# A hybrid MLA and FoX attention layer on one core: nine more places for raw weights during the half-block products, and a new schedule for the sums of w_out's blocks

## The chip, the cores and the metric

One core of a Trainium2 chip runs the kernel; the other cores of the chip are not used. The time of a run is the device time of one execution in microseconds. Before the change three runs took 912.26, 913.48 and 908.7 us, the median is 912.26 us. The profiled execution took 912.14 us, of which the profile's span covers 910.4 us, with a granted TensorE clock of 0.997.

## The reference

One decoder layer with S = 512 positions and D = 2048 columns: an RMS norm, one wide input projection, two attention branches of eight heads each (latent attention, "MLA", and forgetting attention, "FoX"), both with SiLU gates, one output projection, a second RMS norm and the residual.

```python
h = _rms_norm(x, g_pre)
proj = h @ w_in
(q_lat, kv_lat, k_rope_raw, gate_mla,
 fq, fk, fv, f_logit, gate_fox) = jnp.split(proj, split_points, axis=-1)
o_mla = _mla_branch(q_lat, kv_lat, k_rope_raw, g_q, w_uq, g_kv, w_ukv, cos, sin) * jax.nn.silu(gate_mla)
o_fox = _fox_branch(fq, fk, fv, f_logit, b_forget) * jax.nn.silu(gate_fox)
o = jnp.concatenate([o_mla, o_fox], axis=-1) @ w_out
return x + _rms_norm(o, g_post)
```

Both branches are causal softmax attention; FoX adds differences of cumulated forget gates to its logits, MLA gets its heads' queries, keys and values from normed latents by two more projections.

## The kernel before

**Matmuls and chunks.** Every float32 product is made of three matmuls of split operands: the weights' high part by the activations' high part, low by high, and high by low (`mm3`, L137 to L140). A weight matrix is streamed in chunks of 128 x 1024 float32 (0.524 MB). For each chunk SP issues one load into a `raw` tile (`load`), ScalarE casts it to the high part (`whi`, L249), VectorE subtracts this from raw and gets the low part (`wlo`, L250, a "division"), and TensorE takes both. `chunk(i)` loads up to four chunks ahead and divides two ahead. `raw` has three places in the pool `wp`, so a load waits until the third chunk before it is divided.

**The stages**, by chunk number: the FoX heads and, last of them, the projection of the rest of the latents (`lat`, up to 72, its matmuls take 408 to 435 us together with the tails of the last two FoX heads); then the half-block products 73 to 128; the MLA heads 129 to 148; w_out from 149 on.

**The half-block products.** The latents' (`l`) and the MLA gate's (`m`) projections are computed with fewer block products from sums of blocks: p1, p2, p4, then q6, g5, g7, g3. Each product has four chunks for `l` (matmul tiles gl, gbl, then gcl, gdl) and four for `m` (gm, gbm, gcm, gdm): 73 to 76 p1 l, 77 to 80 p1 m, 81 to 88 p2, 89 to 92 p4 l, 93 to 96 p4 m, 97 to 128 the rest. Chunks 89 to 96 are made of two loads: `raw` from a sum in DRAM (t6) and `second` from w_in; VectorE adds them (L246) right before the division.

**Sums of blocks.** The sums are made in DRAM, one step each, 56 in all (`add_step`): SP copies the first block into a tile `t` (L297), POOL accumulates the second block into it with a DMA (L294), and SP writes a mark of 16 numbers from a weight tile into the next `t` (L299), which ties the step to the progress of the products. `paced` starts a step after as many weight blocks as `set_pace` says: every 4 in `lat`, none in the half-block products (1000), every 2 in the MLA heads.

**Other traffic.** POOL writes attention outputs and their gate sums out to DRAM (`awayoa`, `awayog`, `put` at L884), SP fetches operands of products back (`fetch`, L908: bmq, bmg; boa).

**Pools.** `pp` holds the attention heads' own tiles (two places of each), `tb` and `tp` constants and temporary tiles. `inner`, which holds all three, is closed before the output's pool `op` opens, which takes their room.

**Order.** The program is written in TensorE's order; side work (the `todo` queue) is taken out of a queue between matmul groups, `rate` pieces at a time (`pump`). A scheduler then orders the instructions of each engine by its own costs. Each engine and each DMA queue then runs its instructions in that fixed order.

Of the kernel before, what the change touches and what calls it, by code (L numbers as in the profile page):

```python
# [12 lines left out]
F32 = mybir.dt.float32  # L13
# [6 lines left out]
P = 128  # L20
# [22 lines left out]
RND = 12582912.0  # L43
V3 = 3 * HW
NSLOT = 28


def split_const(c, bits, n):
# [15 lines left out]
def tile_hybrid_layer(  # L64
# [16 lines left out]
    nc = tc.nc  # L81
# [5 lines left out]

    inner = ctx.enter_context(ExitStack())
    tb = inner.enter_context(tc.tile_pool(name="tb", bufs=1))
    pp = inner.enter_context(tc.tile_pool(name="pp", bufs=2))  # L90
    tp = inner.enter_context(tc.tile_pool(name="tp", bufs=4))
    dr = ctx.enter_context(tc.tile_pool(name="dr", bufs=1, space=bass.MemoryType.DRAM))
    ps = ctx.enter_context(tc.tile_pool(name="ps", bufs=4, space=bass.MemoryType.PSUM))

    def slot(name, dt=F32, shape=(P, 2, S)):

        return sp.tile(list(shape), dt, tag="s", name=name)
# [4 lines left out]
    def proj_bank(name):  # L102
        return bank("pj", name, 4)
# [90 lines left out]
    chunks = []  # L194
# [11 lines left out]

    raws, ready = {}, {}

    more = []

    def raw_tile(i):
        pool = more[0] if more and (i - more[1]) % 6 < 3 else wp
        return pool.tile([P, 1024], F32, tag="raw", name=f"raw{i}", bufs=3)

    def load(i, small=None):

        w, cols, k, n, width = chunks[i]
        if cols is None:

            raw = raw_tile(i)  # L220
            nc.sync.dma_start(raw, w)
            raws[i] = raw
            if k is not None:
                second = slot(f"second{i}")
                nc.sync.dma_start(second, k)
                raws[i] = raw, second.rearrange("p k c -> p (k c)")
            return
        if i < 2:
            raw = slot(f"raw{i}", shape=(P, 1024))
        else:  # L230
            raw = raw_tile(i)
        v = raw[:, : n * width].rearrange("p (k c) -> p k c", k=n)
        for at, off, cnt in cols:
            (nc.sync if cnt >= P or small is None else small).dma_start(
                v[:, :, at : at + cnt],
                w[0, k * P : (k + n) * P, off : off + cnt].rearrange("(k p) c -> p k c", p=P),
            )
        raws[i] = raw
# [14 lines left out]
    state = {"loaded": 0, "divided": 0, "tiles": 0, "turn": 0, "step": -1, "pace": 6}  # L253
# [4 lines left out]
            state["divided"] += 1  # L258

    def chunk(i, ahead_load=4, ahead=2):  # L260
        while state["loaded"] < min(len(chunks), i + ahead_load + 1):
            load(state["loaded"])
            state["loaded"] += 1
        prepare(i + ahead)
        return ready.pop(i)

    fox = []
    for p in range(4):
        c = {}
# [13 lines left out]
    lat = add_chunks(w_in, [(0, 1024, 256)], NK, 4, 256)  # L283
# [197 lines left out]
    def set_pace(n):  # L481
        state.update(pace=n, tiles=0)
# [17 lines left out]
    def proj_T(rng, outs, kh, kl, rate=1):  # L500

        k = 0
        n_k = sum(chunks[i][3] for i in rng)
        for i in rng:
            hi, lo = chunk(i)
            for j in range(chunks[i][3]):
                for o, rows, pick in outs:
                    mm3(o[:rows, :], pick(hi, j), pick(lo, j), kh[k], kl[k], k == 0, k == n_k - 1)
                k += 1
                pump(rate)  # L510
                behind(hi)
# [406 lines left out]
    def along(a, b):  # L918
        return [lambda x=x, y=y: (x(), y()) for x, y in zip(a, b)]
# [4 lines left out]
    def operand(n, of):  # L924
        def parts(kk, t):
            return [oper[n, of][kk // 2][:, x, kk % 2, t * P : (t + 1) * P] for x in range(2)]

        return parts
# [256 lines left out]
        latents[i] = split(raw(i), f"ln{i}")  # L1185

    todo.append(rotary_key)
    set_pace(4)
    lb = [proj_bank(f"l4{i}") for i in range(2)]
    proj_T(lat, [(lb[i], P, two[i]) for i in range(2)], hh, hl)  # L1190
    while later:
        later.popleft()()
    for i in range(2):
# [15 lines left out]
    def sums_wide(n):  # L1209
        return lambda kk: [oper[n, "m"][kk // 2][:, x, kk % 2, :] for x in range(2)]  # L1210
# [30 lines left out]
    def gate(f, top, bottom):  # L1241

        if f % 2 == 0:
            o_of.append(slot(f"gm{f // 2}"))
        g = o_of[-1][:, f % 2, :]
        pt = att_bank(f"gmt{f}")
        c = slice(f % 4 * P, (f % 4 + 1) * P)
        for t in range(NT):
            pe.transpose(pt[:, t * P : (t + 1) * P], (top, bottom)[t // 2][:, t % 2, c], ident)
        act.activation(g, pt, AF.Tanh)  # L1250
        dve.scalar_tensor_tensor(out=g, in0=g, scalar=1.0, in1=pt, op0=ALU.add, op1=ALU.mult)
        gm.append(g)

    set_pace(1000)
    A, A2 = ([proj_bank(f"g{n}{t}") for t in range(2)] for n in "lm")
    product("p1", "l", x_wide(0, 0), A, True, True, turned=True)
# [22 lines left out]
    scaled(c21, B2, 2, pb)  # L1279
    drain()  # L1280
    C, G = ([proj_bank(f"g{n}l{t}") for t in range(2)] for n in "cd")
    product("q6", "l", sums_wide("q6"), C, True, True, side=[*f5[2:], *along(d5[:2], f7[:2])], turned=True)
    raws_of += [slot(f"lat{i}") for i in (2, 3)]
    lat_sum(lat_block(1, 0), C, pl, ALU.subtract)
# [34 lines left out]
    drain()  # L1319
    for f in range(4, 8):  # L1320
        todo.append(lambda f=f: gate(f, c12, c22))
    qnh, qnl = zip(*(latents[i] for i in range(6)))
    knh, knl = zip(*(latents[i] for i in range(6, 10)))


    for p in range(4):
        c = mla[p]
        if p == 3:
            for f in (*fetches("a11", "o"), *fetches("a12", "o")):
                f()  # L1330
        qb = [proj_bank(f"mq{p}{i}") for i in range(3)]

        proj_T(c["q"], [(qb[i], P, cols(i * P)) for i in range(3)], qnh, qnl, rate=2)
        q = [[split(qb[i], f"mq{p}{i}", SC_M, first=P)] for i in range(2)]
        wholes = slot(f"mw{p}")
        qw = [[whole_block(wholes, i, qb[i], SC_M)] for i in range(2)]
        a, b = rotate(qb[2], P, SC_M, f"q{p}")
        for i in range(2):
            r = tmp(f"rq{p}{i}")
            src = slice(ROPE * i, ROPE * (i + 1))  # L1340
            for half in range(2):
                dve.tensor_tensor(
                    out=r[ROPE * half : ROPE * (half + 1), :], in0=a[src, :], in1=b[src, :], op=ALU.add
                )
            q[i].append(split(r, f"rq{p}{i}", first=P))
            qw[i].append(whole_block(wholes, 4 + i, r))
        if p == 0:
            set_pace(2)
        if p == 3:
            todo.extendleft([*divisions("a11", "o"), *divisions("a12", "o")])  # L1350
        kb = [proj_bank(f"mk{p}{i}") for i in range(2)]
        vb = [proj_bank(f"mv{p}{i}") for i in range(2)]

        def v_cols(w, j):
            return w[:, j, :].rearrange("p (h c) -> p h c", h=2)[:, :, NOPE:]

        kk = 0
        for i in c["kv"]:
            hi, lo = chunk(i)
            for j in range(chunks[i][3]):  # L1360
                fst, lst = kk == 0, kk == KVR // P - 1
                for n in range(2):
                    w = cols(256 * n)
                    mm3(kb[n], w(hi, j), w(lo, j), knh[kk], knl[kk], fst, lst)
                for t in range(NT):
                    o = vb[t // 2][:, (t % 2) * 256 : (t % 2) * 256 + 256]
                    ts = slice(t * P, (t + 1) * P)
                    mm3(
                        o, knh[kk][:, ts], knl[kk][:, ts], v_cols(hi, j), v_cols(lo, j),
                        fst and t % 2 == 0, lst, skip_group_check=True,  # L1370
                    )
                kk += 1
                pump(2)
                behind(hi)
        k = [[split(kb[i], f"mk{p}{i}"), (kr, None)] for i in range(2)]
        kw = [[whole_block(wholes, 2 + i, kb[i]), kr.bitcast(F32)[:, :P]] for i in range(2)]
        drain()
        values_into(v_pair(f"mv{p}"), slice(0, 256), [piece_of(vb, t, 256)[0] for t in range(NT)])
        vs = values_of(f"mv{p}")
        heads = [  # L1380
            Head(
                f"m{2 * p + i}", q[i], k[i],
                vs[i],
                lambda h=2 * p + i: gm[h],
                list(zip(qw[i], kw[i])),
            )
            for i in range(2)
        ]
        enqueue_scores(heads)
        enqueue_values(heads)  # L1390
        done += heads
# [124 lines left out]
            s()  # L1516

    product("p2", 0, operand("a12", "o"), A, False, True, 2, (6, heads_end))
    inner.close()
    op = ctx.enter_context(tc.tile_pool(name="op", bufs=8, reuse_waits="tile"))  # L1520
    more.extend([op, state["loaded"]])
# [88 lines left out]
```

## Time and profile before

| What | us |
|---|---|
| median of three runs | 912.26 |
| lowest and highest | 908.7, 913.48 |
| the profiled execution | 912.14 |
| its span | 910.4 |
| TensorE busy in it | 898.7 |
| VectorE busy | 625.2 |
| ScalarE busy | 424.6 |
| p1, p2 and p4 (chunks 73 to 96) run on TensorE from, to | 436, 505 |
| q6 to g3 (chunks 97 to 128) run from, to | 505, 601 |

TensorE works in 4732 matmuls. A matmul of 512 columns starts 0.23 us after the one before it, one of 256 columns 0.12 us; a larger distance is a wait. In the rows of the trace PE is TensorE, DVE VectorE, ACT ScalarE, and SPq the queue of DMA issues on SP. `out<-in` names the tiles, and a bracket at the end of a row says how long the engine had been idle and what ended that. DMA shares are the mean over the core's 16 DMA engines; 1 is all busy.

### The profile page before, as it was taken

Reading aid. Unit: us, or ns where it says so; the run is one execution under the profiler, and the core shown is the slowest. Engines: PE = TensorE matmul, PEld = TensorE weight load, DVE = VectorE, ACT = ScalarE, POOL = GpSimd, SP = SyncE. Lnnn points to the kernel's source line nnn. Section 1 sums busy time; section 2 is a strip of 40 time slices with the busy share of each in tenths; the row PEclk is TensorE's granted clock in tenths of the full one; section 3 lists DMA queues with packets and bytes.
Section 4 is the critical chain, followed back from the end, with each engine's and each line's share of the span. In section 5 each row is a group of like instructions: output and inputs, shape, how many; then the busy total and the mean of one; then the engine's idle time right before and its main releaser. Section 6 shows DMA issues by size and latency. Waiting matters only on the chain.

```text
span 910.4 us, 12934 instructions
## 1 busy us (share of the span) xinstructions
PE 898.7 (99%) x4732; PEld 774.3 (85%) x4732; DVE 625.2 (69%) x1074; ACT 424.6 (47%) x779; POOL 80.9 (9%) x97
## 2 busy tenths in 40 slices
PE   8999999999999999999999999999999999999997
PEld 8988888898889988888998998878888888888885
DVE  3467778537563684474758777978877986886585
ACT  5773333234222342242464556644554565654483
POOL 1010110110120110111100000001101000000021
PEclk9999999999999999999999999999999999999998
DMA  9378987987898798899798875559999546786878
GB/s 291 96 197 192 250 218 199 231 222 195 231 256 210 200 233 226 228 219 228 228 312 304 289 221 162 162 157 230 215 231 254 117 122 203 243 257 216 278 188 251
DMA packets 121364, 199.40 MB, mean 219 GB/s; under 512 B 16050, under 2 KB 59596, under 8 KB 121300
## 3 DMA queue, kind: packets, MB, share of 16 engines
q1 hardware_dynamic: 105044, 158.84, 55.5%
q0 software_dynamic: 15520, 39.33, 23.5%
q8 instruction: 37, 0.61, 0.3%
q10 hardware_dynamic: 736, 0.40, 0.2%
q14 instruction: 27, 0.22, 0.1%
HBM read 186.46 MB, written 70.80 MB: 283 GB/s over the span
## 4 chain that ended last, share of the span: by engine, by line
PE 92%; DVE 4%; DMA 2%; ACT 1%; issue 1%; SPq 0%; ACTq 0%; DVEq 0%
PE fv L561 4%; PE fg L138 3%; PE fq L140 3%; PE fq L138 3%; PE fq L139 3%; PE fg L140 3%; PE fg L139 3%; PE fk L139 3%; PE fk L140 3%; PE fk L138 3%; PE sm L604 3%; PE fv L140 2%; PE fv L138 2%; PE fv L139 2%; PE mq L138 2%; PE mq L140 2%
## 5 line engine op out<-in xcount | busy, mean ns | idle before, releaser
L250 DVE TENSOR_TENSOR wlo<-raw,whi 128x1024 fp32r<-128x1024 f32 (+3 forms) x205 | 242.8, 1186 | 172.3 <-ACT whi L249 162.2
L249 ACT CAST whi<-raw 128x1024 fp32r<-128x1024 f32 (+3 forms) x205 | 209.4, 1022 | 297.5 <-PE fk L139 52.9
L138 PE MATMUL fq<-h,whi 128*128 128x512 f32 x128 | 52.6, 411 | 0.0
L138 PE MATMUL fg<-h,whi 128*128 128x512 f32 x128 | 51.0, 398 | 0.0
L140 PE MATMUL fq<-h,wlo 128*128 128x512 f32 x128 | 50.3, 393 | 0.0
L139 PE MATMUL fq<-h,whi 128*128 128x512 f32 x128 | 50.1, 391 | 0.0
L140 PE MATMUL fg<-h,wlo 128*128 128x512 f32 x128 | 50.1, 391 | 0.0
L138 PE MATMUL fk<-h,whi 128*128 128x512 f32 x128 | 50.0, 391 | 0.0
L139 PE MATMUL fg<-h,whi 128*128 128x512 f32 x128 | 49.9, 390 | 0.0
L139 PE MATMUL fk<-h,whi 128*128 128x512 f32 x128 | 49.8, 389 | 0.0
L140 PE MATMUL fk<-h,wlo 128*128 128x512 f32 x128 | 49.8, 389 | 0.0
L294 POOL DMA_DIRECT2D t<-in_w_out_dram x16 | 18.5, 1159 | 261.8 <-DMA t<-in_w_out_dram 232.1
L140 PE MATMUL fv<-whi,h 128*128 128x256 f32 (+1 forms) x128 | 39.5, 309 | 0.0
L139 PE MATMUL fv<-wlo,h 128*128 128x256 f32 (+1 forms) x128 | 39.5, 309 | 0.0
L138 PE MATMUL fv<-whi,h 128*128 128x256 f32 (+1 forms) x128 | 39.5, 309 | 0.0
L561 PE MATMUL fv<-whi,h 128*128 128x456 f32 x128 | 38.9, 389 | 0.0
L621 ACT ACTIVATE pf<-sf,stf 128x128 f32<-128x128 f32 (+3 forms) x32 | 16.9, 528 | 26.9 <-DVE stf L619 26.9
L138 PE MATMUL mq<-ln,whi 128*128 128x512 f32 x72 | 28.8, 400 | 0.0
L140 PEld LDWEIGHTS fq<-h,wlo 128*128 128x128 f32 x128 | 24.0, 188 | 5.4
L140 PEld LDWEIGHTS fg<-h,wlo 128*128 128x128 f32 x128 | 24.0, 188 | 5.3
L139 PE MATMUL mq<-ln,whi 128*128 128x512 f32 x72 | 28.3, 393 | 0.0
L140 PEld LDWEIGHTS fk<-h,wlo 128*128 128x128 f32 x128 | 24.0, 188 | 5.0
(525 smaller groups left out, 2456.8 us busy)
## 6 DMA issues: line engine op xcount, KB each, us to landing
raw<-in_w_in_dram SPq DMA_DIRECT2D x80, 512.0 KB
t<-in_w_out_dram SPq DMA_DIRECT2D x32, 512.0 KB
raw<-t SPq DMA_DIRECT2D x32, 512.0 KB
raw<-in_w_out_dram SPq DMA_DIRECT2D x24, 512.0 KB
t<-in_w_out_dram POOLq DMA_DIRECT2D x16, 512.0 KB, 8.5
t<-t POOLq DMA_DIRECT2D x16, 512.0 KB, 7.5
awaymg<-rmg POOLq DMA_DIRECT2D x8, 512.0 KB, 8.6
raw<-t6l SPq DMA_DIRECT2D x8, 512.0 KB
```

The costliest lines, as they stand in the source:

```text
L138: pe.matmul(o, ah, bh, start=first, stop=False, **kw)
L139: pe.matmul(o, ah, bl, start=False, stop=False, **kw)
L140: pe.matmul(o, al, bh, start=False, stop=last, **kw)
L249: act.copy(hi[:, :m], raw[:, :m])
L250: dve.tensor_tensor(out=lo[:, :m], in0=raw[:, :m], in1=hi[:, :m].bitcast(F32), op=ALU.subtract)
L294: pool.dma_start(to.rearrange("p (k c) -> p k c", k=2), second, accum_op=ALU.add)
L561: pe.matmul(banks[t][:, :n], a[k][:, tss[t]], b[:, j, :], start=k == 0 and m == 0, stop=k == NK - 1 and m == 2,)
L604: pe.matmul(s[:, :nn], a[:, qs], c[:, :nn], start=(i == 0), stop=(i == len(pairs) - 1))
L621: act.activation(p, s[:, :n], AF.Exp, bias=st[:, 0:1], accum_out=st[:, 1:2])
```

## The change

The pool `pp` moves into a room of its own, `heads_room`, which is closed before the half-block products. In its place a pool `rw` with nine raw places (`DEEP`) is opened, until the MLA heads open `pp` again. In the products nine of twelve raws take a deep place, three a place of `wp`; the `second` blocks of 89 to 96 take deep places too (before: slots of the general pool). Loads run up to eleven chunks ahead in place of four. In `lat` a sum step comes after every 3 blocks in place of 4, which makes five steps there in place of four, and the side work is pumped at rate 2. From q6 on there is a step after every 8 blocks, eight steps in all (before: none). In the MLA heads the steps come after every 4 blocks in place of every 2, eight steps in place of seventeen.

```diff
+DEEP = 9
...
-    pp = inner.enter_context(tc.tile_pool(name="pp", bufs=2))
     tp = inner.enter_context(tc.tile_pool(name="tp", bufs=4))
+    heads_room = ctx.enter_context(ExitStack())
+    pp = heads_room.enter_context(tc.tile_pool(name="pp", bufs=2))
...
     def raw_tile(i):
+        if deep and deep[1] <= i < deep[2] and (i - deep[1]) % (DEEP + 3) < DEEP:
+            return deep[0].tile([P, 1024], F32, tag="raw", name=f"raw{i}", bufs=DEEP)
...
-                second = slot(f"second{i}")
-                nc.sync.dma_start(second, k)
-                raws[i] = raw, second.rearrange("p k c -> p (k c)")
+                second = deep[0].tile([P, 1024], F32, tag="raw", name=f"second{i}", bufs=DEEP)
+                nc.sync.dma_start(second.rearrange("p (k c) -> p k c", k=2), k)
+                raws[i] = raw, second
...
     def chunk(i, ahead_load=4, ahead=2):
-        while state["loaded"] < min(len(chunks), i + ahead_load + 1):
+        upto = i + ahead_load
+        if deep:
+            upto = max(upto, min(i + DEEP + 2, deep[2] - 1))
+        while state["loaded"] < min(len(chunks), upto + 1):
...
-    set_pace(4)
+    set_pace(3)
     lb = [proj_bank(f"l4{i}") for i in range(2)]
-    proj_T(lat, [(lb[i], P, two[i]) for i in range(2)], hh, hl)
+    proj_T(lat, [(lb[i], P, two[i]) for i in range(2)], hh, hl, rate=2)
...
+    heads_room.close()
+    room = ctx.enter_context(ExitStack())
+    deep.extend(
+        [
+            room.enter_context(tc.tile_pool(name="rw", bufs=DEEP, reuse_waits="tile")),
+            state["loaded"], prods["g3", "m"][-1] + 1,
+        ]
+    )
     set_pace(1000)
...
+    set_pace(8)
     product("q6", "l", sums_wide("q6"), C, True, True, side=[*f5[2:], *along(d5[:2], f7[:2])], turned=True)
...
+    deep.clear()
+    room.close()
+    pp = heads_room.enter_context(tc.tile_pool(name="pp", bufs=2, reuse_waits="tile"))
...
         if p == 0:
-            set_pace(2)
+            set_pace(4)
...
+    heads_room.close()
     inner.close()
     op = ctx.enter_context(tc.tile_pool(name="op", bufs=8, reuse_waits="tile"))
```

The new loads and tiles also change the order in which the scheduler sets VectorE's, SP's and POOL's instructions. In the names below the number after raw, second, whi or wlo is the chunk's; the one behind the underscore is the tile's. The line numbers of the changed kernel are four higher here (L250 is the addition, L254 the division) and seven higher further down.

VectorE at the end of p2 and the start of p4, before:

```order
L250 TENSOR_TENSOR wlo85_4283<-raw85_4208,whi85_4282 128x1024
L130 TENSOR_TENSOR bmq63_4342<-bmq63_4342 128x512
L250 TENSOR_TENSOR wlo86_4315<-raw86_4248,whi86_4314 128x1024
L250 TENSOR_TENSOR wlo87_4353<-raw87_4280,whi87_4352 128x1024
L250 TENSOR_TENSOR wlo88_4375<-raw88_4312,whi88_4374 128x1024
L246 TENSOR_TENSOR raw89_4348<-raw89_4348,second89_4350 128x1024
L130 TENSOR_TENSOR bmg50_4368<-bmg50_4368 128x512
L250 TENSOR_TENSOR wlo89_4398<-raw89_4348,whi89_4397 128x1024
L246 TENSOR_TENSOR raw90_4370<-raw90_4370,second90_4372 128x1024
L130 TENSOR_TENSOR bmg51_4390<-bmg51_4390 128x512
L250 TENSOR_TENSOR wlo90_4419<-raw90_4370,whi90_4418 128x1024
```

Each addition (L246) stands close before its own division, behind the divisions of all the chunks before it. VectorE in p1 m and p2 l, changed:

```order
L254 TENSOR_TENSOR wlo77_4099<-raw77_4014,whi77_4098 128x1024
L254 TENSOR_TENSOR wlo78_4129<-raw78_4016,whi78_4128 128x1024
L254 TENSOR_TENSOR wlo79_4162<-raw79_4018,whi79_4161 128x1024
L250 TENSOR_TENSOR raw89_4177<-raw89_4177,second89_4179 128x1024
L254 TENSOR_TENSOR wlo80_4182<-raw80_4020,whi80_4181 128x1024
L254 TENSOR_TENSOR wlo81_4202<-raw81_4022,whi81_4201 128x1024
L250 TENSOR_TENSOR raw90_4197<-raw90_4197,second90_4199 128x1024
L254 TENSOR_TENSOR wlo82_4222<-raw82_4024,whi82_4221 128x1024
L250 TENSOR_TENSOR raw91_4217<-raw91_4217,second91_4219 128x1024
```

The addition for chunk 89 stands between the divisions of 79 and 80, and those for 90 and 91 alternate with 81 to 83.

SP's DMA issues at the end of `lat`, before (t710 and bmq are a sum step and an operand's fetch):

```order
L234 DMA raw75_3862<-in_w_in_dram 128x2x512
L297 DMA t710_153<-in_w_out_dram 128x2x512
L234 DMA raw76_3916<-in_w_in_dram 128x2x512
L234 DMA raw77_3975<-in_w_in_dram 128x2x512
L234 DMA raw78_4007<-in_w_in_dram 128x2x512
L234 DMA raw79_4041<-in_w_in_dram 128x2x512
L234 DMA raw80_4076<-in_w_in_dram 128x2x512
L234 DMA raw81_4114<-in_w_in_dram 128x2x512
L234 DMA raw82_4134<-in_w_in_dram 128x2x512
L234 DMA raw83_4156<-in_w_in_dram 128x2x512
L234 DMA raw84_4179<-in_w_in_dram 128x2x512
L234 DMA raw85_4208<-in_w_in_dram 128x2x512
```

There bmq60 to bmq63, raw86 to raw88, and only then raw89 and second89 follow. Changed (t510 is the fifth sum step's first block):

```order
L304 DMA t510_165<-in_w_out_dram 128x2x512
L238 DMA raw77_4014<-in_w_in_dram 128x2x512
L238 DMA raw78_4016<-in_w_in_dram 128x2x512
L238 DMA raw76_3947<-in_w_in_dram 128x2x512
L238 DMA raw79_4018<-in_w_in_dram 128x2x512
L238 DMA raw80_4020<-in_w_in_dram 128x2x512
L238 DMA raw81_4022<-in_w_in_dram 128x2x512
L238 DMA raw82_4024<-in_w_in_dram 128x2x512
L238 DMA raw83_4026<-in_w_in_dram 128x2x512
L238 DMA raw84_4028<-in_w_in_dram 128x2x512
L238 DMA raw85_4066<-in_w_in_dram 128x2x512
L238 DMA raw86_4096<-in_w_in_dram 128x2x512
```

It goes on without anything else to raw86, raw87, raw88, raw89 and second89; the operands' fetches stand behind them, and raw77 and raw78 ahead of raw76.

POOL's DMA issues at the same place, before:

```order
L294 DMA t403_148<-t603_144 128x1024
L294 DMA t710_153<-in_w_out_dram 128x2x512
L884 DMA awayoa110_4132<-gf3_3733 256x1x256
L884 DMA awayog51_4074<-rog51_4059 128x1024
L884 DMA awayog31_4109<-rog31_4094 128x1024
L884 DMA awayog50_4177<-rog50_4168 128x1024
L884 DMA awayog30_4200<-rog30_4191 128x1024
L294 DMA t510_165<-in_w_out_dram 128x2x512
L294 DMA t610_157<-t710_153 128x1024
```

and changed:

```order
L891 DMA awayog51_3931<-rog51_3928 128x1024
L891 DMA awayog31_3942<-rog31_3939 128x1024
L301 DMA t403_148<-t603_144 128x1024
L301 DMA t710_153<-in_w_out_dram 128x2x512
L301 DMA t510_165<-in_w_out_dram 128x2x512
L891 DMA awayoa110_3959<-gf3_3733 256x1x256
L891 DMA awayog50_3980<-rog50_3977 128x1024
L891 DMA awayog30_3994<-rog30_3991 128x1024
L301 DMA t610_157<-t710_153 128x1024
```

The accumulation into t510 moved from behind the writes of the gates (L884, now L891) to a place ahead of three of them.

More of the change, by code (lines that the diff above doesn't have):

```diff
@@ L207, in tile_hybrid_layer @@
     raws, ready = {}, {}
-    more = []
+    more, deep = [], []
     def raw_tile(i):
+        if deep and deep[1] <= i < deep[2] and (i - deep[1]) % (DEEP + 3) < DEEP:
+            return deep[0].tile([P, 1024], F32, tag="raw", name=f"raw{i}", bufs=DEEP)
         pool = more[0] if more and (i - more[1]) % 6 < 3 else wp
```

## The prediction

> **What bounds the kernel now.** I read the page's busy shares first, then the list of what TensorE waited for, then the chain of waits around the longest of those.
>
> ```profile
> PE 898.7 (99%) x4732; PEld 774.3 (85%) x4732; DVE 625.2 (69%) x1074; ACT 424.6 (47%) x779; POOL 80.9 (9%) x97
> PE xt L423 <- DVE wlo L250: 1.3, 1, 1.3
> PE gbm L139 <- DVE wlo L250: 1.1, 2, 0.6
> PE sm L604 <- ACT pm L621: 1.0, 1, 1.0
> PE gdm L139 <- DVE wlo L250: 0.7, 1, 0.7
> ```
>
> TensorE is busy for 898.7 us of a span of 910.4 us, so only 11.7 us are there to be won in all, and the change leaves TensorE's instructions as they are. It touches the last three rows alone, beyond start and end of the program. Everything else that it does can only cost, wherever it makes TensorE wait. So the question is whether the new order of the other engines and of the transfers keeps up.
>
> The first stall is p4's m part. The chain there, and TensorE's starts:
>
> ```profile
> 492.00 1.24 DVE wlo L250
> 493.25 0.32 SPq L221
> 493.62 4.34 DMA second<-in_w_in_dram
> 498.06 1.22 DVE raw L246
> 499.28 1.15 DVE wlo L250
> 495.69 0.63 PE L138 MATMUL gbm<-whi,h 128*128 128x512 f32 x2
> 496.83 0.50 PE L139 MATMUL gbm<-wlo,h 128*128 128x512 f32 x1 [0.52 <-DVE wlo L250]
> 499.24 0.63 PE L138 MATMUL gbm<-whi,h 128*128 128x512 f32 x2
> 500.47 0.50 PE L139 MATMUL gbm<-wlo,h 128*128 128x512 f32 x1 [0.61 <-DVE wlo L250]
> ```
>
> A division (wlo) frees a raw place, the place lets the next `second` be fetched, that takes 4.34 us, then comes the addition (1.22) and the next division. Two matmuls of this shape take 0.46 us (0.23 apart), so the two pairs shown lose 1.14 - 0.46 = 0.68 and 1.23 - 0.46 = 0.77 us, **1.45 us** in all.
>
> The second is in the MLA heads:
>
> ```profile
> 693.39 4.41 DMA boa<-awayoa
> 697.80 0.94 DVE wlo L250
> 698.81 7.18 DMA raw<-in_w_out_dram
> 706.04 0.20 ACT pm L621
> 690.00:700.00 10.00, 9.97 (x66) 8.81 (x65) 8.12 (x14) 5.91 (x15) 1.13 (x1) 1.00 1.03 254
> ```
>
> VectorE stands behind a fetch and then a raw that takes 7.18 us, with the DMA engines full (share 1.03); the score matmul sm starts 1.0 us late by the list of waits.
>
> **The change part by part.**
>
> *Additions of p4 (L246).* Before, raw89 and second89 were fetched at 470 and added in the row just ahead of their own division. Now they are loaded eleven chunks ahead. The order of VectorE, quoted with the change, shows what follows: the addition raw89 += second89 stands directly after wlo79 and **ahead of wlo80**, nine divisions early. VectorE runs its instructions in order, so chunk 80's division waits for the landing of second89, and TensorE waits for chunk 80's division. What must be in time:
>
> ```profile
> 446.10 1.23 DVE L250 TENSOR_TENSOR wlo<-raw,whi 128x1024 fp32r<-128x1024 f32 x1 [0.16 <-ACT whi L249]
> 449.27 1.22 DVE L250 TENSOR_TENSOR wlo<-raw,whi 128x1024 fp32r<-128x1024 f32 x1
> 451.89 1.23 DVE L250 TENSOR_TENSOR wlo<-raw,whi 128x1024 fp32r<-128x1024 f32 x1
> 456.00 0.39 PE L138 MATMUL gm<-whi,h 128*128 128x512 f32 x1
> 456.23 0.39 PE L139 MATMUL gm<-wlo,h 128*128 128x512 f32 x1
> 458.72 0.28 PE L138 MATMUL gl<-h,whi 128*128 128x256 f32 x1
> L246 DVE TENSOR_TENSOR raw<-raw,second x8: 1216/1218/1224, 475.4 to 498.1; 128x1024 f32<-128x1024 f32 x8
> ```
>
> The rows are wlo78, wlo79, wlo80, chunk 80's first two matmuls and the first of chunk 81; the second of chunk 80's is the first to use wlo80. So second89 must have landed by 456.23 - 1.23 - 1.22 = **453.8**. Everything that VectorE must still do stands behind that addition.
>
> When does it land? In SP's new order thirteen transfers of 0.524 MB that before were issued at 440.26 or later stand ahead of it or are it: raw78 to raw85 (the x8 of the first row), raw86 to 88, raw89 and second89.
>
> ```profile
> 440.26 18.64 SPq L234 DMA_DIRECT2D raw<-in_w_in_dram  x8
> 462.88 4.92 SPq L234 DMA_DIRECT2D raw<-in_w_in_dram  x3
> 470.50 0.37 SPq L225 DMA_DIRECT2D second<-in_w_in_dram  x1
> 416.00:430.00 14.00, 14.00 (x70) 11.59 (x69) 4.54 (x6) 3.66 (x7) 2.84 (x3) 1.00 0.96 237
> 430.00:440.00 10.00, 10.00 (x63) 8.98 (x62) 5.64 (x8) 4.63 (x9) 1.29 (x2) 1.00 0.47 118
> 440.00:450.00 10.00, 10.00 (x77) 9.62 (x76) 9.69 (x13) 5.06 (x7) 0.53 (x1) 1.00 0.92 300
> 475.00:480.00 5.00, 5.00 (x23) 4.13 (x22) 4.41 (x5) 2.30 (x3) 0.00 (x0) 1.00 1.03 406
> q1 hardware_dynamic: 105044, 158.84, 55.5%
> q0 software_dynamic: 15520, 39.33, 23.5%
> ```
>
> In the windows the columns before the last two are busy times and clock; the last two are DMA share and GB/s. The best stretch of loads alone, 475 to 480, moves 406 GB/s at a share of 1.03: 0.524 MB / 406 GB/s = 1.29 us a transfer. The stretch with sums in it, 416 to 430, moves 237 GB/s at the same fullness, so the software queue's bytes cost more engine time: by the queue table 0.235 x 910.4 us / 39.33 MB x 0.524 MB = 2.85 us for 0.524 MB, against 0.555 x 910.4 / 158.84 x 0.524 = 1.67 for SP's.
>
> With the pace of 3 a fifth step of sums falls into the latents' projection: its copy (t510) stands in SP's queue just ahead of raw77, its accumulation in POOL's, with two 0.524 MB writes of gates and one of 0.262 MB behind it. That gives, from 440 on:
> - 13 + 1 transfers of SP x 1.29 = 18.1 us;
> - 3.5 transfers of POOL's at 1.29 to 2.85 = 4.5 to 10.0 us;
> - less what the engines have free from 430 to 440, (1 - 0.47) x 10 = 5.3 us, if the attention's room is left in time for loads to run there;
> - plus the way from the last byte to the semaphore. A lone second takes 4.34 us, of which 1.29 is transfer; of the 3.05 left I take half, 1.5 us, since issue overlaps the queue.
>
> Sum: 440 + 17.3 + 1.5 = 458.8 to 440 + 22.8 + 1.5 = 464.3, middle 461.5. TensorE then goes on at 461.5 + 1.22 + 1.23 = 464.0 in place of 456.23: **a stall of 7.8 us** (5.0 to 10.5). Bounds beyond: second89 uses the place of raw78 and can't be issued before that chunk's division, which ended at 446.10 + 1.23 = 447.3; with the lone transfer's 4.34 it lands at 451.7 at the earliest, in time, stall 0. At the price of 1.67 for all of SP's it is 5.3 later than with 1.29, stall 16.
>
> The Trainium skill, page "DMA: Bandwidth & Descriptors", section "Specifications", sets the HBM limit of a core at about 358 GB/s. By that the fourteen would take 20.5 us in place of 18.1 and the stall would be 2.4 us longer. This case's row with 406 GB/s lies above that limit, so the measurement decides.
>
> What comes after that stall: the additions of 90 to 96 have alternated into the divisions of 81 to 88, their `second`s arrive one behind another 2 x 1.29 = 2.6 us apart, and a chunk keeps TensorE from 456.00 to 458.72, 2.7 us. So the transfers just keep up, and I cost the rest of p1, p2 and p4 at nothing more. The cover is small: at 1.67 it would be 3.3 us a pair and eight chunks would lose 0.6 us each, 5 us. In p4 itself both operands are then long there, so the 1.45 us go: **-1.5** (bounds -1.1, the list's figure, and -2, with the first matmuls of each chunk).
>
> *The latents' projection at rate 2.* The tail of the last attention heads is pumped twice as fast. From 416 to 430 VectorE is busy for 4.54 and ScalarE for 3.66 of 14 us, so it fits on average; short waits where a head's operand comes behind a division are possible. I take **+0.4**, bounds 0 and one division, 1.2. raw76 now stands behind raw77 and raw78 in SP's queue: up to 2 x 1.29 = 2.6 late against a reserve that I can't read closely; counted in the range only.
>
> *Eight sum steps beside q6 to g3.* There were none there.
>
> ```profile
> 546.00:614.00 68.00, 67.34 (x341) 56.24 (x340) 56.78 (x94) 38.71 (x57) 0.00 (x0) 1.00 0.55 161
> ```
>
> Eight steps need 8 x (1.29 + 2.85) = 33 us of the DMA engines; the window alone leaves 0.45 x 68 = 31 free, and the nine places ahead absorb the rest. Cost 0; without the cover a load late by a step's 4.1 us would be hidden still by eleven loaded chunks. gdm's 0.7 us wait lies there and stays: VectorE is busy for 56.78 of 68 us with the same instructions.
>
> *Fewer sums beside MLA.* Eight steps in place of seventeen take 9 x 4.1 = 37 us of transfers out of a stretch that is full, so boa and the raw at 698.81 come sooner: **-0.9** of the 1.0 us (bounds 0, -1.2).
>
> *Rooms closed and opened* (before MLA and before the output's pool) wait for tiles last used long before; 0, within 0 to +1.
>
> Sum: 912.14 + 7.8 - 1.5 + 0.4 - 0.9 = 917.9. The profiled execution's 912.14 us (span 910.4 and 1.7 around it) is 0.1 us under the median, so this stands for the median too: **917.9 us**, +0.6%. With the stall of 5.0 to 10.5 it is 915.1 to 920.6.
>
> **The rivals.**
>
> *In time (no stall).* If loads start early enough in the latents' projection, and POOL's writes stand behind them, second89 lands by 453.8 and the addition costs VectorE nothing, since it idles elsewhere. Then only the gains are left: 912.14 - 1.5 - 0.9 = 909.7, and at most, with the bounds -2 and -1.2 and gdm's 0.7 by a lead in divided chunks, 908.2. For it: share 0.47 just before 440, and the earliest landing of 451.7. Against it: from 440 to 450 the engines are 0.92 full already with much less to move. It decides from 3 us of TensorE's time, which is what the gains can pay. This is the case that ends below before.
>
> *Part of it.* POOL's accumulation moves behind the loads, the landing is 455 to 458, the stall 1 to 4 us: 912.14 + 2.5 - 2.4 + 0.4 = 912.6, no change that can be told.
>
> *Worse.* With 1.67 us a transfer the stall is 13 to 16 and raw76 is late too: 912.14 + 13 - 2.0 + 1 = 924.
>
> *It doesn't start early.* If the room of the attention came free only late, all loads would begin there and the stall would be longer still. The last matmuls that read its tiles:
>
> ```profile
> L646 PE MATMUL pvf<-pdf,fv x4: 270/273/275, 423.9 to 436.2; 128*128 128x128 f32 x4
> ```
>
> They start at 436.2 at the latest, and come earlier at rate 2, so I fold this into the one before.
>
> **How the numbers follow.** The forecast's chance is 0.5, in time 0.2, part of it 0.2, worse 0.1. The range, 908.5 to 923, holds the forecast's whole own range (915.1 to 920.6), the part case, most of the first rival and a little of the worse one. This kernel can be told from no change beyond about 0.5%, 4.6 us: faster is below 907.7, slower above 916.8. Slower: four fifths of the forecast's 0.5, all of the worse 0.1, a little of the part case's upper end, 0.54. Faster: the first rival reaches 908.2 by its own terms, so only if places won somewhere unseen, 0.13 with unknowns elsewhere in the order. The rest, 0.33, is no change.
>
> **What would show it.** Right: a wait of gm's second matmul in chunk 80 (L141 there) of 5 to 10 us for VectorE's wlo, behind the addition (L250 there), which itself waits for the DMA of `second`, at 456 to 465; DMA share about 1 from 440 to 462; no gbm wait in p4; sm's wait of 1.0 gone and a lower DMA share beside MLA. Wrong: no wait of TensorE between 450 and 470 (then second89 landed by 454, and the sum of transfers from 440 was too long), or a stall already at chunk 76 or 77, when the nine places open late.

## The result, and the profile after

The changed kernel takes 918.4 us (median of six runs, 917.21 to 921.32) against 911.48 us of before in the same comparison (six runs, 908.7 to 913.48): a ratio of 1.0083, with an interval of 1.0061 to 1.0105. It is slower by about 7 us, and the interval leaves out 1. The profiled execution took 917.21 us, its span is 915.4 us.

The engines' row of the page, and the waits that matter from the list of what TensorE waited for (us in total, times, longest):

```profile
PE 898.5 (98%) x4732; PEld 775.2 (85%) x4732; DVE 625.0 (68%) x1074; ACT 423.8 (46%) x779; POOL 80.9 (9%) x97
PE gm L141 <- DVE wlo L254: 6.8, 1, 6.8
PE gl L140 <- ACT whi L253: 0.8, 1, 0.8
PE gl L142 <- DVE wlo L254: 0.8, 1, 0.8
PE gdm L141 <- DVE wlo L254: 0.7, 1, 0.7
```

TensorE's 4732 matmuls are the same; the waits are others. Those of gbm (p4) and sm (MLA) are gone, gdm's is as it was, and one of 6.8 us has come in p1 m, with two of 0.8 us shortly before it. The chain there (start, duration, what):

```profile
448.06 0.74 DVE wlo L254
448.80 10.91 DMA second<-in_w_in_dram
459.89 1.08 issue
460.97 1.23 DVE wlo L254
462.25 0.79 PE gm L141
463.04 0.43 PE gm L142
```

and VectorE at the same time:

```profile
448.06 1.23 DVE L254 TENSOR_TENSOR wlo<-raw,whi 128x1024 fp32r<-128x1024 f32 x1 [0.84 <-ACT whi L253]
459.83 1.23 DVE L250 TENSOR_TENSOR raw<-raw,second 128x1024 f32<-128x1024 f32 x1 [10.54 <-DMA second<-in_w_in_dram]
460.97 2.35 DVE L254 TENSOR_TENSOR wlo<-raw,whi 128x1024 fp32r<-128x1024 f32 x2
```

VectorE ends wlo79 at 449.3 and then idles for 10.54 us in front of the addition for chunk 89, until second89 has landed; wlo80 follows, and TensorE's second matmul of chunk 80 starts at 462.25. Chunk 80's own raw had landed long before: ScalarE casts it at 449.85. The DMA engines and the clock in windows (the last three columns are granted clock, DMA share and GB/s):

```profile
430.00:440.00 10.00, 10.00 (x72) 9.42 (x71) 4.63 (x7) 2.99 (x5) 2.61 (x4) 1.00 1.08 285
440.00:450.00 10.00, 8.45 (x56) 7.51 (x55) 5.50 (x5) 5.73 (x8) 0.00 (x0) 1.00 1.04 402
450.00:460.00 10.00, 5.48 (x25) 4.20 (x23) 0.17 (x1) 3.00 (x3) 0.00 (x0) 0.99 0.86 326
455.00:462.20 7.20, 0.48 (x3) 0.06 (x1) 2.37 (x3) 1.04 (x1) 0.00 (x0) 0.83 0.50 185
462.20:464.00 1.80, 1.75 (x4) 1.47 (x5) 1.13 (x1) 0.00 (x0) 0.00 (x0) 0.50 0.89 274
464.00:466.40 2.40, 2.40 (x7) 1.81 (x7) 1.63 (x2) 0.34 (x1) 0.00 (x0) 0.50 1.01 364
```

From 430 to 450, where before had a share of 0.47 and 0.92, the engines are full. Towards the end of the wait they empty (0.50 from 455 to 462.2): the next second uses second89's place and is issued at 461.08, when the addition has read it, so SP's queue stood still too. The last two rows show what the forecast's sum didn't have: after the wait TensorE works at half its clock, and matmuls of 512 columns start 0.43 us apart in place of 0.23, until 466.4. So not every distance above 0.23 us is a wait; this one is the clock.

From p1's first matmul (436.2 before, 433.3 after) to the end of the span the change takes 482.1 us against 474.2, 7.9 more. The rows give 6.8 for the wait; 2.1 for the half clock (eleven matmuls from 462.25 to 466.85 in 4.60 us, which at 0.228 take 2.5); 1.6 for the two waits of chunk 76; less 1.5 in p4 and 1.0 in MLA: 8.0. That p1 starts 2.9 us earlier in this execution belongs to the program's beginning, which differs from execution to execution (before has a wait of xt of 1.3 us there, this one none; the second group of fv's matmuls starts at 12.22 us in before and at 9.43 here), so the two spans lie closer together than the medians.

### The profile page after: what moved, and what is told of

The parts are those of the page before. It is cut to its first block, busy times and chain, and to the rows that moved or that the text cites. A ratio compares the mean times of both kernels' runs of the same rounds, so it can differ in the third digit from the quotient of the medians.

```text
span 915.4 us, 12935 instructions
## 1 busy us (share of the span) xinstructions
PE 898.5 (98%) x4732; PEld 775.2 (85%) x4732; DVE 625.0 (68%) x1074; ACT 423.8 (46%) x779; POOL 80.9 (9%) x97
## 4 chain that ended last, share of the span: by engine, by line
PE 92%; DMA 4%; DVE 2%; ACT 1%; issue 0%; SPq 0%; ACTq 0%; DVEq 0%
PE fv L568 4%; PE fg L140 3%; PE fq L142 3%; PE fq L140 3%; PE fq L141 3%; PE fg L142 3%; PE fg L141 3%; PE fk L141 3%; PE fk L140 3%; PE fk L142 3%; PE sm L611 3%; PE fv L141 2%; PE fv L142 2%; PE fv L140 2%; DMA raw<-in_w_in_dram 2%; PE mq L140 2%
## 5 line engine op out<-in xcount | busy, mean ns | idle before, releaser
L254 DVE TENSOR_TENSOR wlo<-raw,whi 128x1024 fp32r<-128x1024 f32 (+3 forms) x205 | 242.5, 1185 | 158.5 <-ACT whi L253 155.4
L301 POOL DMA_DIRECT2D t<-t x16 | 13.4, 839 | 258.0 <-DMA t<-in_w_out_dram 210.2
```

Source lines behind the costliest of these rows:

```text
L254: dve.tensor_tensor(out=lo[:, :m], in0=raw[:, :m], in1=hi[:, :m].bitcast(F32), op=ALU.subtract)
L301: pool.dma_start(to.rearrange("p (k c) -> p k c", k=2), second, accum_op=ALU.add)
```

## The experiments

The theory: VectorE runs in order, the addition for chunk 89 stands nine divisions too early, and TensorE waits for as long as second89 is late for that place. The rivals: the crowd of transfers delays raw80 and its neighbours anyway, or the fifth sum step or the rate costs the time in other ways.

**The addition on GpSimd.**

```diff
-            dve.tensor_tensor(out=raw, in0=raw, in1=second, op=ALU.add)
+            pool.tensor_tensor(out=raw, in0=raw, in1=second, op=ALU.add)
```

> The eight additions of raw and second run on GpSimd instead of VectorE; the order of the loads is the same. Theory (the addition blocks VectorE): second89 still lands near 460, but wlo80 no longer stands behind it, so TensorE's wait of 6.8 us at chunk 80 and the 2.1 us of matmuls at half clock behind it go: 918.4 - 8.9 = 909.5 us. Rival (the crowded queue itself: raw80 and the raws behind it are late too): a wait of 5 us or more stays between 450 and 465, 915 us or more. A GpSimd addition slower than 2.7 us each would show as waits in p4, 480 to 505.

Measured: 922.68 us, ratio 1.0114 (1.0093 to 1.0134). Half of the theory held: from 450 to 460 TensorE is busy for 10.00 us, and there is no wait at chunk 80, so raw80 was there and it is the addition that had blocked it. But another wait of 8.2 us came at 470, which neither side had expected: the time lies in the rival's range, the wait not where the rival had it. Its chain:

```profile
461.06 3.33 POOL raw L250
464.41 3.68 DMA second<-in_w_in_dram
468.31 2.38 POOL raw L250
471.14 0.39 SPq L229
471.62 4.64 DMA bmq<-awaymg
476.27 0.63 ACT bmq L131
478.61 1.22 DVE wlo L254
```

A GpSimd addition takes 2.3 to 3.3 us. The next second is issued only when that addition has ended (its end frees the place), SP's queue stands there, the fetch of bmq (an operand of a later product) stands behind it, and on ScalarE the cast of bmq stands ahead of the next whi: ScalarE idled for 14.28 us in front of that cast. So the additions hold up a second in-order queue, SP's, which had the same order of loads as in the change.

**Only the seconds late again.** They are loaded four chunks ahead into slots of the general pool, by a new function `load_second`; the raws are loaded eleven ahead.

```diff
-                second = deep[0].tile([P, 1024], F32, tag="raw", name=f"second{i}", bufs=DEEP)
-                nc.sync.dma_start(second.rearrange("p (k c) -> p k c", k=2), k)
-                raws[i] = raw, second
+                raws[i] = raw, k
...
+        if deep:
+            load_second(i + 4)
```

> Only the second blocks are fetched four chunks ahead again (into slots as before the change); the raws keep their nine places and eleven chunks of lead. Theory: the additions stand beside their own divisions again, the wait at chunk 80 goes, and of the waits in p4 (1.9 us before) some come back, since the addition again waits for a late second: 909.5 to 911.5 us. Rival (nine places alone crowd the queue): the wait at chunk 80 stays with 5 us or more, 915 us or more.

Measured: 911.6 us, ratio 1.0 (0.9983 to 1.0017). The wait at chunk 80 is gone, and 0.8 and 0.4 us came back at p4. Nine places for the raws, with eleven chunks of lead, don't make the stall by themselves.

**Seven and nine chunks ahead** (the same edit with another number).

> As changed, with the pace of 3 and rate of 2 of the change, but the second blocks are fetched seven chunks ahead instead of eleven (into slots of their own, as in the run with four). The addition for chunk 89 stands behind wlo84, five places later. Theory (place of the addition): no wait at chunk 80 and none at 85, raw76's late landing stays with up to 1.6 us, p4 has no waits since the seconds come earlier than with four: 918.4 - 9.0 = 909.4 us (908 to 911). Rival (rate 2 and pace 3 cost the time by other ways): 914 us or more.

> The same with nine chunks ahead: the addition for chunk 89 stands behind wlo80, one place later than in the change, and one more load (raw90) stands ahead of second89. Theory: second89 lands at about 461, the addition and wlo81 end at 463.6, and TensorE needs wlo81 at about 459: a wait of 4 to 5 us at chunk 81, then 1.5 to 2 us of matmuls at half clock: 914 to 917 us. Rival (the place doesn't matter): the wait stays at chunk 80 with 7 us, or is gone as with seven.

Measured: 909.39 us with seven (0.9975, 0.9959 to 0.999) and 916.36 with nine (1.0053, 1.0033 to 1.0073). With nine the addition stands one division later than in the change, and the wait moves by one chunk, to the low part of chunk 81:

```profile
PE gl L142 <- DVE wlo L252: 6.3, 2, 5.5
```

5.5 of the 6.3 us are that wait. With seven the addition starts at 468.14 and finds its second landed; no wait of TensorE over 0.8 us is left in p1 to p4.

**The latents' projection as before**, the rest as changed.

```diff
-    set_pace(3)
+    set_pace(4)
...
-    proj_T(lat, [(lb[i], P, two[i]) for i in range(2)], hh, hl, rate=2)
+    proj_T(lat, [(lb[i], P, two[i]) for i in range(2)], hh, hl)
...
-    set_pace(8)
+    set_pace(7)
```

> In the latents' projection the pace of 4 and the rate of 1 are as before the change (the missing sum step goes beside the last eight products, pace 7); the rest is as changed. The addition for chunk 89 then stands behind wlo82 instead of wlo79. Theory (what counts is how far ahead of its data the addition stands): three chunks or 8 us later, about when second89 lands, so a wait of 0 to 2 us at chunk 83 and none at 80: 909.5 to 911.5 us. Rival (the transfers of the nine places and not the place of the addition): the wait stays with 5 us or more wherever it then stands, 915 us or more.

Measured: 906.56 us, ratio 0.9944 (0.9925 to 0.9963), 3 us better than expected and faster than both kernels. VectorE:

```profile
456.59 1.23 DVE L254 TENSOR_TENSOR wlo<-raw,whi 128x1024 fp32r<-128x1024 f32 x1 [1.50 <-ACT whi L253]
460.26 1.23 DVE L250 TENSOR_TENSOR raw<-raw,second 128x1024 f32<-128x1024 f32 x1 [2.44 <-DMA second<-in_w_in_dram]
461.40 1.22 DVE L254 TENSOR_TENSOR wlo<-raw,whi 128x1024 fp32r<-128x1024 f32 x1
```

Here second89 lands no earlier than in the change (the addition starts at 460.26 against 459.83), but the addition stands behind wlo82 in place of wlo79, and TensorE doesn't wait at all from p1 to p4. The pair isn't quite clean: in SP's queue raw76 comes first again, and raw86 stands ahead of raw77. The rows of before account for 2.5 us of the gain (p4's 1.5 and MLA's 1.0; both waits are missing here); from p1's first matmul to the end of the span it is 3.6 us, and the rest isn't explained. The two parts one at a time:

> As changed, but with the pace of 4 in the latents' projection (one sum step fewer there; pace 7 from q6 on makes up for it). The addition for chunk 89 stands behind wlo79 as in the change. Theory (place of the addition against the landing of second89): one copy of 1.3 us and one accumulation of up to 2.9 us fewer ahead of second89, it lands at 456 to 458 instead of 459.8, so the wait at chunk 80 is 3 to 5 us instead of 6.8, with some matmuls at half clock behind it: 913 to 916.5 us. Rival (the fifth step itself made the stall): no wait there, 908 us or less.

> As changed, but with rate 1 in the latents' projection; the fifth sum step stays there. The addition for chunk 89 stands behind wlo82. Theory: second89 lands some 3 us later than without the fifth step (460.2), at about 463, the addition and wlo83 end at 465.5, TensorE needs wlo83 at about 464.5: a wait of 0 to 3 us, 906.5 to 910 us. Rival (the fifth step makes the stall): a wait of 5 us or more, 912 us or more.

Measured: 914.78 us with the old pace alone (1.0028, 1.0011 to 1.0044) and 908.23 with the old rate alone (0.9961, 0.9947 to 0.9975), both inside what was expected. With the old pace the addition still stands behind wlo79, and its second lands 5 us earlier than in the change:

```profile
454.62 1.23 DVE L250 TENSOR_TENSOR raw<-raw,second 128x1024 f32<-128x1024 f32 x1 [7.40 <-DMA second<-in_w_in_dram]
```

TensorE's wait at chunk 80 is 3.6 us. Raw76 doesn't hold TensorE here, so it asks for wlo80 at 453.4, sooner than in the change; the earlier landing didn't save the whole 5 us.

| run | addition of 89 behind | it starts at | longest wait of gl, gm | us |
|---|---|---|---|---|
| the change | wlo79 | 459.83 | 6.8, chunk 80 | 918.4 |
| old pace, rate 2 | wlo79 | 454.62 | 3.6, chunk 80 | 914.78 |
| seconds nine ahead | wlo80 | 461.65 | 5.5, chunk 81 | 916.36 |
| old pace and rate | wlo82 | 460.26 | none | 906.56 |
| pace 3, old rate | wlo82 | 461.50 | 0.9 | 908.23 |
| seconds seven ahead | wlo84 | 468.14 | 0.8 | 909.39 |

**Before, with the new schedule of sums alone.**

```diff
+    set_pace(7)
     product("q6", "l", sums_wide("q6"), C, True, True, side=[*f5[2:], *along(d5[:2], f7[:2])], turned=True)
...
-            set_pace(2)
+            set_pace(4)
```

> The kernel before with only the new schedule of sums behind p4: nine steps beside the last eight products (pace 7), the MLA heads at pace 4; no deep places, the latents' projection as before. Theory: the wait of sm at 705 goes, p4's waits stay: 0.9 to 1.2 us less than before, 910.4 us (910 to 911). Rival 1: the steps beside the products delay loads there, which have only four chunks of lead here: no gain or a loss, 911.5 us or more. Rival 2: more than 2 us of gain, and the nine places give little of the 906.6 us that the change makes with the old latents' projection.

Measured: 922.78 us, ratio 1.0113 (1.0085 to 1.0141): a loss, rival 1 in a size that it hadn't. The chain in q6 to g3:

```profile
549.35 8.93 DMA raw<-t6m
558.38 1.06 ACT whi L249
559.47 1.23 DVE wlo L250
560.69 1.81 DVE ls L1151 x3
562.55 1.36 PE lbq L1161 x8
565.62 0.64 PE gcm L138
566.26 0.43 PE gcm L139
```

A raw takes 8.93 us to land between the sums' transfers (from 552 to 565 the DMA share is 1.02); four chunks of lead don't cover it, VectorE and with it the latents' statistics (lbq) are late, and TensorE's next matmuls are 0.43 us apart. It isn't the only stall: at 604.87 the list has another wait of 2.1 us, of gmt for VectorE. The wait of sm is gone, so the schedule of sums alone removes it. With nine places the same steps stand beside the same products, and the list of the run with the old projection has only gdm's 0.7 us left there.

**Zeros in the wait.** Matmuls of zeros, added to chunk 80's sums ahead of chunk 80.

```diff
+            if (name, g) == ("p1", "m") and i == rng[-1]:
+                for n in range(FILL):
+                    pe.matmul(o[0][:, :P], warm, warm, start=False, stop=False, skip_group_check=True)
```

> 26 matmuls of zeros onto chunk 80's sums stand ahead of chunk 80; at 0.25 us each (as the 12 at the program's start) they fill 6.5 of the 6.8 us that TensorE waits. Theory on the half clock (it follows TensorE's own idleness): the ten matmuls after the wait start 0.23 apart in place of 0.43, 2.1 us less, 916.3 us. Rival (it follows something else at that time, such as the full DMA engines or the restart of VectorE): they stay 0.43 apart, 918.4 us or, if the zeros overrun the wait, more.

> As the run with 26 matmuls of zeros, but 12 of them, about 2.8 us: TensorE idles some 4 us at chunk 80 instead of 6.8 or 1.9. Theory (a stretch of idleness between 1.9 and 6.8 us long halves the clock): whether the matmuls after it are 0.43 or 0.23 apart narrows this length; I expect 0.43 for a part of them. Rival (the zeros' own low activity or something else decides): no half clock at 4 us and also none at later long waits of this run.

Measured: 926.26 us with 26 (1.0164, 1.0141 to 1.0188), 921.23 with 12 (one run). Neither time is what was expected, but the clock is. With 26, in windows:

```profile
459.20:461.50 2.30, 0.43 (x3) 0.12 (x2) 2.30 (x3) 0.00 (x0) 0.00 (x0) 1.00 0.12 21
461.50:464.00 2.50, 2.48 (x11) 2.07 (x12) 1.10 (x1) 0.34 (x1) 0.00 (x0) 1.00 0.93 297
470.30:478.90 8.60, 0.00 (x0) 0.00 (x0) 3.62 (x4) 1.69 (x3) 0.00 (x0) 0.77 0.77 250
478.90:481.80 2.90, 2.88 (x13) 2.88 (x14) 2.90 (x5) 1.73 (x3) 0.00 (x0) 0.51 0.86 275
```

The wait at chunk 80 shrinks to 1.9 us, and chunk 80's matmuls run at 1.00 (second row). A new wait of 8.6 us stands in p2, and behind it the clock is halved again. The zeros have also changed VectorE's order: the additions for 92 and 93 stand ahead of wlo83 here, in the change behind it (that of 93 behind wlo85). So TensorE's wait for wlo83 is the same kind of stall one place on:

```profile
471.19 1.23 DVE L251 TENSOR_TENSOR raw<-raw,second 128x1024 f32<-128x1024 f32 x1 [2.30 <-DMA second<-in_w_in_dram]
476.50 1.22 DVE L251 TENSOR_TENSOR raw<-raw,second 128x1024 f32<-128x1024 f32 x1 [4.08 <-DMA second<-in_w_in_dram]
477.65 2.35 DVE L255 TENSOR_TENSOR wlo<-raw,whi 128x1024 fp32r<-128x1024 f32 x2
```

So the time of this run doesn't price the half clock; its windows show when it comes. With 12, TensorE idles for 5.7 us, and the clock behind it is 0.50 for 3.8 us.

## Why the prediction was right, and where its terms were off

**The stall** was the forecast's main term, 7.8 us at chunk 80's second matmul; it is there, in that place, behind that addition, with 6.8 us. second89 was expected at 461.5 and the addition started at 459.83, inside the 458.8 to 464.3 of the sum. It was issued at 448.80, a little behind the bound of 447.3 that its place sets, and took 10.91 us to land in the crowd, where a lone second takes 4.34. The place is shown as the cause by three things: with the same order of loads and the addition on GpSimd the wait at chunk 80 is gone; with nearly one landing and two places (459.83 and 460.26) the times are 918.4 and 906.56 us; and with nine chunks the wait follows the addition by one chunk, with seven it is gone. One sign came only in part: the DMA share was to be about 1 until 462, and from 455 on it was 0.50.

**The half clock** was missing: 2.1 us. **raw76** was in the range only and cost two waits of 0.8, 1.6 us. The order of raw77 and raw78 ahead of it isn't enough to make them: the runs with the seconds four and seven chunks ahead have the same order there, and waits of 0 and 0.2 us; what else it takes is open. The forecast's terms make +5.8; by the rows the change is +8.0: 1.0 less in the stall, 0.4 less for the rate, 0.1 more from MLA, and 3.7 from these two. The medians lie 6.9 apart; the 1 us between that and the rows isn't explained (single runs of before spread over 4.8 us). So 917.9 for 918.4 is luck in part: the mechanism and the place were right, but terms that were too high and terms that were missing offset each other.

**p4** gave its 1.5 and **MLA** 1.0 (0.9 forecast), shown by the missing rows gbm and sm. Beside MLA, the windows of before and of the change:

```profile
600.00:780.00 180.00, 178.85 (x984) 153.64 (x983) 142.05 (x285) 95.23 (x215) 14.90 (x15) 1.00 0.76 199
```

```profile
600.00:780.00 180.00, 179.24 (x990) 154.11 (x989) 144.70 (x289) 95.50 (x216) 6.77 (x7) 1.00 0.54 142
```

The share falls from 0.76 to 0.54 with eight sums fewer in the stretch.

**The rate of 2** was the step that was mis-sized in its role. It was costed by itself, at +0.4 us for short waits; no such wait is in the list. But the rate is what sets the addition's place: at rate 2 it stands behind wlo79 with either pace, at the old rate behind wlo82 with either pace (the loads of raw76 and raw86 move too), and with pace 3 that one edit makes 918.4 into 908.23 us. Pace 3 makes the landing later, and its undoing alone gives 3.6 us. I had read the place from the order and priced it rightly without asking which edit had put it there. That the scheduler moves it because the attention's tail and with it the room end earlier is argued, not shown.

**The eight sum steps** beside the products were costed at nothing, with the nine places' lead as the cover. With the places that held: gdm's 0.7 us is the only wait left there. But the cover is worth more than the 4.1 us of a step that the prediction names: the run without the places lost 10 us (922.78 against 912.47). So the sums beside the products need the places. What the places give without the sums was not run, and the gain of 0.56% (906.56 us) is that of both together, once the additions stand late enough.

## What to carry to other kernels

More buffers and earlier loads change the in-order queues of the engines that consume them: when an operation on late data is set ahead of work that is due now, the whole lead turns into a stall. After such a change, look up for each moved wait what stands behind it in the same queue, on the compute engine and on the issuing one, and compare its landing with the first use of what is behind; taking the operation to another engine (GpSimd here) only moves the wait if the queue of loads is tied to it too. Where a change has two halves, run each alone: here one half costs 10 us without the other (the other half alone was not run), and a setting in a third place, the rate, decided the sign.

## What the runs showed of the hardware

A wait of TensorE has a second price. After waits of 3.6, 5.5, 5.7, 6.8 and 8.6 us (in the change and four of the experiments) the granted clock was 0.50 for 3 to 5 us, which costs half of that again; after the wait of 1.9 us it stayed at 1.00. After the 8.2 us of the run with GpSimd it was 0.50 for 6.4 us, with another wait of 1.2 us inside. Little work can count as a wait: in the run with the sums' schedule alone a wait of 2.2 us and sixteen matmuls of one column, 3 us long, were also followed by matmuls 0.43 us apart. The Trainium skill, page "TensorE: Matmul & The Clock Gate", section "What's actually happening", says that a window of about 3.4 us without activity halves the clock, and that as long a busy one restores it, the window running freely. These runs agree: the shortest wait by itself that was followed by the half clock is 3.6 us, and but for the one of 6.4 the stretches at half clock, 2.9 to 5.3 us, lie around that length. By it a wait longer than such a window is priced some 2 us higher, as an estimate half of one to one and a half windows, which would have made the forecast's stall 9.8 us.

A two-input addition of 128 x 1024 float32 took 2.34 to 3.32 us on GpSimd, and 1.22 on VectorE.
